# Ten of eleven gated activation chunks transposed by DMAs instead of TensorE

## The chip, the core and the metric

The kernel runs on one core of a Trainium2 chip. The core has five engines that work side by side, each through its own queue in order: TensorE (PE in the profile; its weight loads are PEld), VectorE (DVE), ScalarE (ACT), GpSimd (POOL) and SyncE (SP, which here only issues DMAs). Sixteen DMA engines move data between the main memory and the core's two on-chip memories, SBUF and, for matmul results, PSUM; a DMA can be issued from the queue of SP, ACT or POOL. The metric is the device time of one execution in microseconds; lower is better.

## What is computed

One layer of a decoder block on a sequence of 256 positions with 2048 channels: a mixer with three kinds of attention, then a gated feed-forward part with 5632 hidden channels. All data is 32-bit floating point. The change lies in the feed-forward part:

```python
h2 = rmsnorm(x, g_ffn)
gu = h2 @ w_gu
x = x + (jax.nn.silu(gu[..., :D_FF]) * gu[..., D_FF:]) @ w_down
```

The gated activation, `silu(...) * ...`, has 256 rows (positions) and 5632 columns. It comes out of the first product with positions on the 128 partitions. The second product, with `w_down`, needs it as the stationary operand, with hidden channels on the partitions: it has to be transposed.

## The kernel before

Every product of two 32-bit matrices is made of three matmuls on a rounded 32-bit format: each operand is split into a high half (rounded by a cast on ACT) and a low half (the rest, a subtraction on DVE), and high x high, high x low and low x high are added up in PSUM (`split`, L105; `product`, L158 to L162). Weights are streamed from the main memory in tiles of two 128-row blocks by 512 columns (`load`, L278, and its `fetch` on SP's queue), split by `parts` (L284) into `w_hi` and `w_lo`, of which there are five buffers each, and used by PE. Raw weights have four buffers (`w_raw`) and, for those that are added to each other, six (`g_raw`).

The gate-and-up loop (L933) goes over eleven chunks of 512 hidden channels. `project_pair` (L318) makes the four results of a chunk (two blocks of 128 positions by gate and up). For half of the depth it uses a form of Strassen's scheme with seven products (`form`) in place of eight, for which DVE adds weight tiles to each other (`u`, L303 and L314), and plain products for the other half (`rest`). A chunk takes 22 calls of `parts`, so 22 splits: four for a pair of forms that the previous chunk begins early (`begin_pair`, L308), then two for form 5, one plain, two for form 6, two plain, two for form 7, one plain, two for form 3, two plain, two for form 4, two plain, and the next chunk's four.

After a chunk's products, ACT makes `silu` (L938) and DVE the product with the up part (L939), for two blocks `sg[0]` and `sg[1]` of 128 positions by 512 channels. `to_a` (L925) then transposes each: four PE transposes of 128 x 128 into one PSUM tile (`transpose4`, L178), a copy to SBUF on ACT (L929), and a DMA from POOL's queue to `a_mem` in the main memory (L930), from which the last part of the kernel, the product with `w_down`, reads it back (L950). Small tiles of 2 KB a partition, such as `sg` and these copies, come from one pool of twelve buffers, `scratch`, through `half_kb` (L89).

What is put in between is written as generators: `stages` is a list that `parts` advances by one step at every split, and `slow_stages` one that it advances by one step at every second split (L288 to L291). So `to_a` does one block at the first split of the next chunk's own program and the other at the second.

The order of each engine's queue is not the order of the program: a planner orders the instructions by a simulated timeline, and where several are ready it takes the one that was written first. `tc.keep_in_program_order` binds an instruction behind everything that was written before it for the same engine; what is written later may still overtake it where it is ready sooner.

Of the kernel before, what the change touches and what calls it, by code (L numbers as in the profile page):

```python
# [8 lines left out]

F32 = mybir.dt.float32  # L10
F32R = mybir.dt.float32r
AF = mybir.ActivationFunctionType
ALU = mybir.AluOpType
AX = mybir.AxisListType
# [3 lines left out]
P = 128  # L18
D = 2048
S = 256  # L20
NT = S // P
# [7 lines left out]
NB = 512  # L29
# [25 lines left out]
def hybrid_block(ctx: ExitStack, tc: tile.TileContext, x, g_mix, w_in, q_gain, k_gain, w_branch, w_out,  # L55
                 g_ffn, w_gu, w_down, rel_bias, onehot, extra, out):
    nc = tc.nc
# [21 lines left out]
    def pool(stack, name, side, bufs=1):  # L79
        return stack.enter_context(tc.tile_pool(name=name, bufs=bufs, side=side, reuse_waits="tile"))  # L80
# [5 lines left out]
    scratch = pool(ctx, "scratch", "right", 12)  # L86
    gx = pool(pgx, "gx", "right", 2)

    def half_kb(dt=F32):  # L89

        return scratch.tile([P, NB], dt, name="sc")
# [13 lines left out]
    def split(hi, lo, src, pin=False):  # L105
        for op in nc.scalar.copy(hi, src), nc.vector.tensor_sub(lo, src, hi.bitcast(F32)):  # L106
            if pin:
                tc.keep_in_program_order(op)

    def raw_weights(w, row0, c, col0):  # L110
        raw = wpool.tile([P, 2, NB], F32, name="w_raw", bufs=4)
        src = w[row0 + c * P: row0 + (c + 2) * P, col0: col0 + NB].rearrange("(k p) n -> p k n", p=P)
        return raw, nc.sync.dma_start(raw, src)

    def weights(w, row0, k0, nk, col0, there=()):

        for i, c in enumerate(range(k0, nk, 2)):
            raw = there[i] if i < len(there) else raw_weights(w, row0, c, col0)[0]
            hi = wpool.tile([P, 2, NB], F32R, name="w_hi")
            lo = wpool.tile([P, 2, NB], F32R, name="w_lo")  # L120
            split(hi, lo, raw)
# [4 lines left out]
    stages, slow_stages = [], []  # L126

    def advance(queue):
        while queue:
            try:  # L130
                next(queue[0])
                return
            except StopIteration:
                queue.pop(0)

    def finish_stages(queue):
        while queue:
            advance(queue)
# [25 lines left out]
    def rsqrt_mean(dst, ss, n, cols):  # L164
# [3 lines left out]
        y = small.tile([P, cols], F32, name=f"rs_y{cols}")  # L168
        nc.scalar.activation(y, v, AF.Ln)
        nc.scalar.activation(y, y, AF.Exp, scale=-0.5)  # L170
        t = small.tile([P, cols], F32, name=f"rs_t{cols}")
# [6 lines left out]
    def transpose4(src):  # L178

        pt = tr.tile([P, 4, P], F32, name="tr")  # L180
        for i in range(4):
            nc.tensor.transpose(pt[:, i, :], src[:, i * P:(i + 1) * P], ident)
        return pt


    class Columns:


        def __init__(self, pl, name, nk):
            self.hi, self.lo = (pl.tile([P, nk, S], F32R, name=f"{name}_{n}") for n in ("hi", "lo"))  # L190

# [20 lines left out]
    class Sums:  # L212
# [8 lines left out]
        def place(self, pl, c):  # L221
            self.s[c] = [pl.tile([P, 4, S], F32R, name=f"{self.name}_s{n}{c}") for n in ("hi", "lo")]

# [14 lines left out]
    class Chunks(Sums):  # L238
# [9 lines left out]
        def place(self, pl, c):  # L248
            if c in self.wc:
                super().place(pl, c)  # L250
                self.t[c] = [[pl.tile(sh, F32R, name=f"{self.name}_{t}{n}{c}") for n in ("hi", "lo")]
                             for t, sh in enumerate(([P, 4, P], [P, 2, P]))]
            else:
                self.t[c] = [pl.tile([P, 4, S], F32R, name=f"{self.name}_{n}{c}") for n in ("hi", "lo")]

# [149 lines left out]
    def to_h(acts, src, c, t, g, by_scalar=False):  # L405

        pt = transpose4(src)
        tmp = half_kb().rearrange("p (k q) -> p k q", k=4)
        if by_scalar:
            for i in range(4):  # L410
                nc.scalar.activation(tmp[:, i], pt[:, i], AF.Copy, scale=g[:, 4 * c + i:4 * c + i + 1])
        else:
            nc.vector.tensor_mul(tmp, pt, g[:, 4 * c:4 * c + 4, None].to_broadcast([P, 4, P]))
        acts.put(c, t, tmp)
        return tmp

    def squares(xc, dst, c, pin=False):
        for t in range(NT):
            sq = nc.scalar.activation(half_kb(), xc[t], AF.Square, accum_out=dst[:, t, c:c + 1])
            if pin:  # L420
# [85 lines left out]
    with tc.manual_schedule(engines={mybir.EngineType.PE, mybir.EngineType.DVE, mybir.EngineType.Activation}):  # L506
# [14 lines left out]
        low_high(0, 1)  # L521
        high_low(0, 1)
        turned = [transpose4(xs[1][0])]
        high_high(1, 0)
        high_high(1, 1)
# [7 lines left out]
        high_high(0, 2)  # L533
        low_high(0, 2)
        turned.append(transpose4(xs[1][1]))
        high_high(1, 2)
        low_high(1, 2)
# [89 lines left out]
    def stick_breaking(hl, qT, kT, v):  # L627
# [7 lines left out]
        l = pa.tile([P, n], F32, name="p", bufs=1)  # L635
        nc.scalar.activation(l, z[:, :n], AF.Abs)
        nc.scalar.activation(l, l, AF.Exp, scale=-1.0)
        nc.scalar.activation(l, l, AF.Ln, bias=1.0)
# [160 lines left out]
    def pair_of(kind, what):  # L799
        if kind == "qk":  # L800
            return hs, w_in, what * NB, NH * HD + what * NB
        if kind == "gates":
            return hs, w_in, gate_col(*what[0]), gate_col(*what[1])
# [16 lines left out]
    for (kind, what), after in zip(units, units[1:] + [(None, None)]):  # L820
# [7 lines left out]
        nxt = pair_of(*after)  # L828
# [94 lines left out]
    a_mem = dram.tile([NF // 4, P, 4, S], F32, name="a_mem")  # L923

    def to_a(c, srcs):  # L925
        for t in range(NT):
            pt = transpose4(srcs[t])
            st = half_kb().rearrange("p (k q) -> p k q", k=4)
            nc.scalar.copy(st, pt)  # L929
            nc.gpsimd.dma_start(a_mem[c, :, :, t * P:(t + 1) * P], st)  # L930
            yield

    for c in range(D_FF // NB):  # L933
        nxt = (h2, w_gu, (c + 1) * NB, D_FF + (c + 1) * NB) if c + 1 < D_FF // NB else None
        (g0, g1_, u0, u1), ahead = project_pair(h2, w_gu, c * NB, D_FF + c * NB, ahead, nxt)
        sg = [half_kb() for _ in range(NT)]
        for t, (g, u) in enumerate(((g0, u0), (g1_, u1))):
            nc.scalar.activation(sg[t], g, AF.Silu, scale=rstd2[:, t:t + 1])  # L938
            nc.vector.scalar_tensor_tensor(sg[t], u, rstd2[:, t:t + 1], sg[t], op0=ALU.mult, op1=ALU.mult)  # L939
        stages.append(to_a(c, sg))  # L940

    WD = (4, 6, 8)
    ORDER = [0, 1, 2, 4, 3, 6, 5, 8, 7, 9, 10]
# [153 lines left out]
```

## Time and profile before

| | us |
|---|---|
| median of three runs | 1434.75 |
| lowest and highest | 1433.64, 1435.78 |
| the profiled execution's own time | 1433.64 |
| its span, first to last instruction | 1431.9 |
| PE busy | 1421.7 |
| DVE busy | 1196.0 |
| ACT busy | 882.0 |

A page of the profile lists one execution. A row of a group of instructions has line, engine, operation, tiles (result <- operands), shapes, how many, busy time in us and the mean of one in ns, and then the engine's idle time just before them and what ended it. A row of a timeline has start and duration in us, then the instruction; in brackets the idle time before it and who ended it. Matmuls overlap in their pipeline, so the distance between two starts, not the duration, is what one costs. The loop of the eleven chunks lies from about 735 to 1196 us of the span.

### The profile page before, as it was taken

The page shows a single profiled execution, that of the slowest core. Times are in us where ns is not written, and L with a number is a line of the kernel's source. Part 1 is how long each engine was busy: PE and PEld are TensorE (multiplying, and loading weights), DVE is VectorE, ACT ScalarE, POOL GpSimd, SP SyncE. Part 2 cuts the span into 40 slices and gives each one's busy share as a digit, 9 for nine tenths or more (in the row PEclk, how much of TensorE's full clock was granted, in tenths as well). Part 3 has the DMA queues.
Part 4 walks back from the last instruction along what each step waited for, and adds up shares of the span by engine and source line. Part 5 has one row for each costly group of instructions (what it writes and reads, how often), then busy time and mean ns, then how long its engine had stood idle before and what let it go on. Part 6 is the DMA issues. An engine that isn't in the chain of part 4 may idle for free. (4 is left out here: it accounts for less than half of the span.)

```text
span 1431.9 us, 17773 instructions
## 1 busy us (share of the span) xinstructions
PE 1421.7 (99%) x6404; PEld 1172.1 (82%) x6404; DVE 1196.0 (84%) x1262; ACT 882.0 (62%) x1140; POOL 72.6 (5%) x133
## 2 busy tenths in 40 slices
PE   9999999999999999999999999999999999999998
PEld 7888888888788888888888888888888888788887
DVE  7888787857999886776689999999999998886775
ACT  7667876766766665444456666666666666554453
POOL 1000000000000002100100000000000010100000
PEclk9999999999999999999999999999999999999999
DMA  8763647465666758866786657666665666767552
GB/s 270 264 218 119 220 127 247 122 221 173 215 203 238 257 194 291 278 224 211 223 299 224 224 206 251 216 225 229 219 217 191 231 212 223 256 230 240 190 169 97
DMA packets 154472, 310.09 MB, mean 217 GB/s; under 512 B 10672, under 2 KB 12288, under 8 KB 154384
## 3 DMA queue, kind: packets, MB, share of 16 engines
q1 hardware_dynamic: 143200, 275.29, 57.1%
q0 software_dynamic: 10000, 32.62, 6.5%
q10 hardware_dynamic: 1184, 1.06, 0.2%
q8 instruction: 50, 0.82, 0.2%
q14 instruction: 38, 0.31, 0.1%
HBM read 292.65 MB, written 16.27 MB: 216 GB/s over the span
## 5 line engine op out<-in xcount | busy, mean ns | idle before, releaser
L106 DVE TENSOR_TENSOR w_lo<-w_raw,w_hi 128x1024 fp32r<-128x1024 f32 x334 | 406.0, 1221 | 91.1 <-ACT w_hi L106 87.5
L106 ACT CAST w_hi<-w_raw 128x1024 fp32r<-128x1024 f32 x334 | 349.0, 1052 | 166.1 <-PE qs L162 67.4
L106 ACT CAST w_hi<-g_raw 128x1024 fp32r<-128x1024 f32 x184 | 192.6, 1053 | 120.4 <-PE ps L162 39.4
L106 DVE TENSOR_TENSOR w_lo<-g_raw,w_hi 128x1024 fp32r<-128x1024 f32 x184 | 219.6, 1220 | 36.1 <-ACT w_hi L106 35.2
L106 ACT CAST w_hi<-u 128x1024 fp32r<-128x1024 f32 x138 | 144.9, 1053 | 136.1 <-DVE u L303 65.1
L106 DVE TENSOR_TENSOR w_lo<-u,w_hi 128x1024 fp32r<-128x1024 f32 x138 | 166.5, 1221 | 37.0 <-ACT w_hi L106 35.6
L161 PE MATMUL ps<-w_lo,h_hi 128*128 128x512 f32 x360 | 140.9, 392 | 0.0
L162 PE MATMUL ps<-w_hi,h_lo 128*128 128x512 f32 x360 | 140.5, 390 | 0.0
L160 PE MATMUL ps<-w_hi,h_hi 128*128 128x512 f32 x360 | 137.5, 393 | 0.0
L161 PE MATMUL qs<-w_lo,h_hi 128*128 128x512 f32 x332 | 130.0, 392 | 0.8 <-DVE w_lo L106 0.8
L162 PE MATMUL qs<-w_hi,h_lo 128*128 128x512 f32 x332 | 129.6, 390 | 0.0
L160 PE MATMUL qs<-w_hi,h_hi 128*128 128x512 f32 x332 | 126.7, 391 | 0.0
L303 DVE TENSOR_TENSOR u<-u,g_raw 128x1024 f32<-128x1024 f32 x80 | 94.4, 1218 | 0.0
L162 PEld LDWEIGHTS ps<-w_hi,h_lo 128*128 128x128 f32 x360 | 67.6, 188 | 14.0
L161 PEld LDWEIGHTS ps<-w_lo,h_hi 128*128 128x128 f32 x360 | 67.6, 188 | 13.7
L160 PEld LDWEIGHTS ps<-w_hi,h_hi 128*128 128x128 f32 x360 | 67.5, 188 | 13.7
L161 PEld LDWEIGHTS qs<-w_lo,h_hi 128*128 128x128 f32 x332 | 62.4, 188 | 13.9 <-DVE w_lo L106 1.2
L162 PEld LDWEIGHTS qs<-w_hi,h_lo 128*128 128x128 f32 x332 | 62.4, 188 | 13.4 <-issue 0.6
L160 PEld LDWEIGHTS qs<-w_hi,h_hi 128*128 128x128 f32 x332 | 62.3, 188 | 12.7
L314 DVE TENSOR_TENSOR u<-g_raw 128x1024 f32<-128x1024 f32 x40 | 48.8, 1219 | 21.0 <-DMA g_raw<-in_w_in 16.2
L160 PE MATMUL v<-w_hi,h_hi 128*128 128x512 f32 x120 | 47.5, 396 | 0.2 <-ACT w_hi L106 0.2
L161 PE MATMUL v<-w_lo,h_hi 128*128 128x512 f32 x120 | 47.1, 393 | 0.0
(397 smaller groups left out, 2935.2 us busy)
## 6 DMA issues: line engine op xcount, KB each, us to landing
w_raw<-in_w_in SPq DMA_DIRECT2D x118, 512.0 KB, 4.6
g_raw<-in_w_gu SPq DMA_DIRECT2D x88, 512.0 KB, 5.1
w_raw<-in_w_gu SPq DMA_DIRECT2D x88, 512.0 KB, 6.4
g_raw<-in_w_in SPq DMA_DIRECT2D x72, 512.0 KB, 5.8
w_raw<-in_w_down SPq DMA_DIRECT2D x64, 512.0 KB, 4.6
w_raw<-in_w_branch SPq DMA_DIRECT2D x32, 512.0 KB, 5.1
w_raw<-in_w_out SPq DMA_DIRECT2D x32, 512.0 KB, 4.7
g_raw<-in_w_down SPq DMA_DIRECT2D x24, 512.0 KB, 5.3
```

What stands on the lines that cost most here:

```text
L106: for op in nc.scalar.copy(hi, src), nc.vector.tensor_sub(lo, src, hi.bitcast(F32)):
L160: nc.tensor.matmul(ps, ah, wh, start=start, stop=False, **how)
L161: nc.tensor.matmul(ps, ah, wl, start=False, stop=False, **how)
L162: nc.tensor.matmul(ps, al, wh, start=False, stop=stop, **how)
L303: tc.keep_in_program_order(nc.vector.tensor_add(d, d, a))
L314: nc.vector.tensor_add(d, a, b)
```

## The change

Chunks 0 to 9 are transposed without PE; chunk 10 stays as it was. The transposing DMA is given 16-bit elements: each 32-bit block is handled as two planes of 16-bit halves:

- `turn_out`: a copy on ACT reads the block as 16-bit numbers and writes all first halves of the words to one plane and all second halves to another (128 x 512 x 2); then a transposing DMA, issued from ACT's queue, turns the eight 128 x 128 blocks of the two planes around. Both are bound to program order.
- `turn_in`: a copy on ACT joins the two turned planes into 32-bit words again, bound to program order too. Then POOL stores the block to `a_mem` as before.
- `to_a_by_dma` is put into `slow_stages` in place of `stages`: first block out, two splits later second block out, then two empty steps, then the first block in (eight splits after it went out) and, two splits later, the second.

Three tiles of `scratch` are used for each block in place of one. Before the last chunk's `to_a`, `slow_stages` is run to its end.

```diff
+U16 = mybir.dt.uint16
...
+    def turn_out(src):
+
+        halves = scratch.tile([P, 2, NB], U16, name="sc")
+        tc.keep_in_program_order(nc.scalar.copy(halves, src.bitcast(U16).rearrange("p (n b) -> p b n", b=2)))
+        turned = scratch.tile([P, 8, P], U16, name="sc")
+        tc.keep_in_program_order(nc.scalar.dma_start_transpose(turned, halves.rearrange("p b n -> p (b n)")))
+        return turned
+
+    def turn_in(turned):
+
+        dst = half_kb().rearrange("p (k q) -> p k q", k=4)
+        tc.keep_in_program_order(nc.scalar.copy(dst.bitcast(U16).rearrange("p k (q b) -> p b k q", b=2),
+                                                turned.rearrange("p (b k) q -> p b k q", b=2)))
+        return dst
...
+    def to_a_by_dma(c, srcs):
+        turned = []
+        for t in range(NT):
+            turned.append(turn_out(srcs[t]))
+            yield
+        yield
+        yield
+        for t in range(NT):
+            nc.gpsimd.dma_start(a_mem[c, :, :, t * P:(t + 1) * P], turn_in(turned[t]))
+            yield
...
-        stages.append(to_a(c, sg))
+        if nxt:
+            slow_stages.append(to_a_by_dma(c, sg))
+        else:
+            finish_stages(slow_stages)
+            stages.append(to_a(c, sg))
```

## The prediction

> **What bounds the kernel now.** First the page: which engine has no idle time.
>
> ```profile
> span 1431.9 us, 17773 instructions
> PE 1421.7 (99%) x6404; PEld 1172.1 (82%) x6404; DVE 1196.0 (84%) x1262; ACT 882.0 (62%) x1140; POOL 72.6 (5%) x133
> ```
>
> PE is never free, so only work taken from PE, or a wait put on it, moves the time. The transposes in question run in the gate-and-up loop of eleven chunks (L933). So next the stretches of that view, one for each chunk; this is one of them, with its columns.
>
> ```profile
> core 0: us, PE busy (x) PEld busy (x) DVE busy (x) ACT busy (x) POOL busy (x), PEclk, DMA share, GB/s
> 986.70:1028.40 41.70, 41.70 (x190) 34.57 (x189) 38.82 (x36) 26.58 (x31) 1.46 (x2) 1.00 0.63 215
> ```
>
> A chunk takes 41.7 us, all PE. DVE is busy 38.8 of it, 93%, and can make up for little; ACT 26.6. PE is fed by a chain: ACT casts a pair of weight rows to its high half (L106), DVE subtracts to get the low half, PE multiplies. There are 22 such splits in a chunk and five buffers for the halves, so what matters is how far ahead the chain is at the place where the change puts its work. I number the splits of a chunk's program from the cast of u after the two pairs begun early: 1 and 2 are u for form 5, 3 a plain row pair, 4 and 5 the new u for form 6, and so on. The timelines of the three engines there (start, duration):
>
> ```profile
> 986.80 0.72 ACT L938 ACTIVATE sc<-sc,rstd 128x512 f32<-128x512 f32 x1
> 987.43 0.67 ACT L938 ACTIVATE sc<-ps,rstd 128x512 f32<-128x512 f32 x1
> 988.00 1.04 ACT L106 CAST w_hi<-u 128x1024 fp32r<-128x1024 f32 x1
> 988.93 0.58 ACT L298 COPY sc<-qs 128x512 f32<-128x512 f32 x1
> 989.48 1.05 ACT L106 CAST w_hi<-w_raw 128x1024 fp32r<-128x1024 f32 x1
> 992.86 0.59 ACT L929 COPY sc<-tr 128x512 f32<-128x512 f32 x1 [2.33 <-PE tr L182]
> 993.34 1.05 ACT L106 CAST w_hi<-u 128x1024 fp32r<-128x1024 f32 x1
> 994.29 0.59 ACT L929 COPY sc<-tr 128x512 f32<-128x512 f32 x1
> 994.77 1.06 ACT L106 CAST w_hi<-u 128x1024 fp32r<-128x1024 f32 x1
> ...
> 988.08 1.41 DVE L939 SCALAR_TENSOR_TENSOR sc<-sc,rstd 128x512 f32<-128x512 f32 x2
> 989.40 1.22 DVE L106 TENSOR_TENSOR w_lo<-u,w_hi 128x1024 fp32r<-128x1024 f32 x1
> 990.57 1.23 DVE L106 TENSOR_TENSOR w_lo<-w_raw,w_hi 128x1024 fp32r<-128x1024 f32 x1
> 991.71 2.36 DVE L303 TENSOR_TENSOR u<-u,g_raw 128x1024 f32<-128x1024 f32 x2
> 994.43 1.23 DVE L106 TENSOR_TENSOR w_lo<-u,w_hi 128x1024 fp32r<-128x1024 f32 x1 [0.36 <-ACT w_hi L106]
> ...
> 995.88 0.39 PE L160 MATMUL qs<-w_hi,h_shi 128*128 128x512 f32 x1
> 996.10 0.39 PE L161 MATMUL qs<-w_lo,h_shi 128*128 128x512 f32 x1
> ```
>
> Split 4 is cast at 993.34, its low half ends at 994.43 + 1.23 = 995.66, and PE reads it at 996.10. **The lead is 0.44 us**, here, just behind the two activations that the change turns out. ACT's one large hole, 2.33 us up to 992.86, lies here too; it is a wait for PE's transposes.
>
> **What is taken away.** Ten chunks lose eight transposes each. In order of time on PE:
>
> ```profile
> 992.23 0.60 PE L182 MATMUL tr<-ident,sc 128*128 128x128 f32 x4
> 992.58 0.48 PE L160 MATMUL z<-w_hi,h_shi 128*128 128x512 f32 x1
> 992.90 0.60 PE L182 MATMUL tr<-ident,sc 128*128 128x128 f32 x4
> 993.25 0.48 PE L160 MATMUL v<-w_hi,h_hi 128*128 128x512 f32 x1
> 993.57 0.40 PE L161 MATMUL z<-w_lo,h_shi 128*128 128x512 f32 x1
> ```
>
> From 992.23 to 993.57 are 1.34 us with two matmuls in them; matmuls follow each other every 0.226 us (995.88 to 996.10). The eight transposes therefore hold PE 1.34 − 0.45 = 0.89 us, and ten chunks 8.9 us. That is all there is to gain. ACT loses two copies a chunk, at a pitch of 0.48 (994.29 to 994.77), and no longer waits for PE.
>
> **What is added on ACT.** Per chunk two copies into planes, two transposing DMAs issued from ACT's own queue, and two copies that join the planes. No such copy is in this trace. It has 1024 elements of 16 bits: the rows above give 0.59 for 512 elements and 1.05 for 1024, so 0.59 if time goes with bytes, 1.05 if with elements. I take 1.05 (0.95 in pitch, 988.00 to 988.93): the two 128x512 forms and the 128x1024 cast lie on one line in the count of elements. ACT's total per chunk becomes 26.6 − 1.0 + 4 × 0.95 = 29.4 and is no bound by itself.
>
> The DMA is the open price. It stands in program order right behind the copy whose result it reads, on the same queue, so ACT cannot start the next cast until the copy has ended and the DMA is issued. I call that hold h. The rows nearest to it are plain DMAs:
>
> ```profile
> L1065 ACTq DMA_DIRECT2D out<-sc x8: 338/338/369, 1307.1 to 1428.6; - x8
> L103 SPq DMA_DIRECT2D g_raw<-in_w_gu x10: 367/368/838, 981.1 to 1024.0; - x10
> L930 POOL DMA_DIRECT2D a_mem<-sc x22: 709/713/825, 785.3 to 1207.2; - x22
> ```
>
> ACT's own stores are 128 runs of 1 KB and take 0.338 us to issue, SP's loads 256 runs of 2 KB and 0.368. A transposed half tile has 128 rows of eight blocks, each block going to another plane: 1024 runs. Straight through the two rows that is 0.338 + 7 × 0.030 = 0.55; in proportion to SP's runs 4 × 0.368 = 1.47. POOL's store of 512 runs, at 0.713, lies between the two lines. To each comes the end of the copy that the DMA waits for, some 0.2, an estimate from the 0.44 between the copy's end at 993.45 and the store's start at 993.89 on another engine:
>
> ```profile
> 993.89 0.73 POOL L930 DMA_DIRECT2D a_mem<-sc  x1 [35.98 <-ACT sc L929]
> ```
>
> So h lies between 0.34 (the plain issue alone) and about 1.7. I take 1.47 + 0.2 = 1.67: by the number of its runs, 1024, the transpose is nearest to SP's row of 256, and a row whose every run goes on to the next address may be cheap for a reason that a transpose does not share.
>
> [...]
>
> **How it adds up at split 4.** Without transposes PE would read split 4's low half 0.89 earlier, at 995.21. ACT now does, after the snapshot that starts at 988.93 (next free at 989.45): copy, hold, cast of split 3, copy, hold. Three pitches of 0.95 and two holds end at 992.3 + 2h, where split 4 can start; not before 992.9 though, when DVE has its first sum of u (991.71 + half of 2.36). Against 993.34 now that is a delay of 2h − 1.04. PE's reading moves by this delay less the lead of 0.44: **each chunk changes by 2h − 1.48 us, and by −0.89 at best**. Break-even is h = 0.74. With 1.67 a chunk is 1.86 us longer, of which PE waits 2.75.
>
> A second order of the same work: if the first copy and its DMA stand ahead of split 3's cast, split 3's low half slips by 0.95 + h, DVE's sums of u behind it in its queue slip as well, and split 4 starts at about 993.85 + h; the chunk changes by h + 0.07, or 1.74 with 1.67. For a long hold both orders agree, and I need not know which one the planner chose.
>
> **What is added later in the chunk.** The joining copies stand behind splits 9 and 11:
>
> ```profile
> 1000.70 2.19 ACT L106 CAST w_hi<-g_raw 128x1024 fp32r<-128x1024 f32 x2 [1.08 <-DVE g_raw L303]
> 1002.78 1.05 ACT L106 CAST w_hi<-w_raw 128x1024 fp32r<-128x1024 f32 x1
> 1003.74 1.04 ACT L106 CAST w_hi<-g_raw 128x1024 fp32r<-128x1024 f32 x1
> 1005.64 1.05 ACT L106 CAST w_hi<-g_raw 128x1024 fp32r<-128x1024 f32 x1 [0.85 <-ACT w_hi L106]
> 1006.98 0.39 PE L160 MATMUL v<-w_hi,h_hi 128*128 128x512 f32 x1
> ```
>
> Split 10 (cast at 1002.78, low half done 2.5 us later, at 1005.28) is first read by PE at 1006.98: a lead of 1.70 against one copy of 0.95. I cost both joins at nothing; if the lead were gone, they would cost up to 1.9 a chunk. Queued behind a join that has to wait for its DMA would be every cast to come, and so DVE and PE. The cover is about 12 us, from an issue near 990.5 to 1002.8. Nearest rows, medians from issue to landing in this stage:
>
> ```profile
> w_raw<-in_w_gu SPq DMA_DIRECT2D x76, 512.0 KB, 6.2
> a_mem<-sc POOLq DMA_DIRECT2D x20, 256.0 KB, 2.5
> ```
>
> 2.5 to 6.2 us fit into 12, so I cost the landing at nothing. [...] POOL's stores to a_mem are the same twenty, some 9 us later; their reader for chunk 9 comes a whole chunk later. The DMA engines are at 0.63 of their time in the chunk and get twice 256 KB more. The twelve scratch buffers have about six holders at this place, so no buffer is late.
>
> **The sum.** 10 × 1.86 = +18.6 on the profiled execution's own 1433.64 us (its span is 1431.9): 1452.2. The median of the runs before is 1434.75, 1.1 above it: **1453 us**.
>
> **Rivals.** *A short hold (the other side).* The issue costs what a plain one costs, h = 0.34 to 0.6, split 3 goes first, and PE keeps most of the 0.89: −1.48 + 2h is −0.80 to −0.28, in ten chunks −8 to −3, 1427 to 1432 us; −8.9 at best. It decides from h below 0.74. For it: issuing hardly grows with bytes (0.338 and 0.368), and ACT's hole of 2.33 us is free for it. Against: the copy's end must be waited for, and the runs are eight times as many.
>
> *A short hold, first copy ahead of split 3.* h + 0.07 with 0.55 is +0.6, ten times +6: 1441. With h near 0.2 it is no change.
>
> *The transposes land late, or hold up the weights.* DMA is full just when they start:
>
> ```profile
> 989.00:991.00 2.00, 2.00 (x10) 1.65 (x10) 2.00 (x3) 1.54 (x3) 0.00 (x0) 1.00 0.98 369
> 991.00:993.00 2.00, 2.00 (x13) 1.65 (x12) 2.00 (x3) 0.14 (x1) 0.00 (x0) 1.00 0.37 132
> ```
>
> If landing took 20 us, ACT would stand 8 us before the first join, PE 8 − 1.7 = 6.3, ten chunks 63 us on top of −8.9 to +19: about 1490 to 1520. It decides from a landing above some 13.7 us. Against it: the share falls to 0.37 from 991 on.
>
> **Chances.** A hold of 1.2 to 2.2 us (each chunk +0.9 to +2.9, so 1444 to 1464): 0.45, the forecast. The short hold with a gain: 0.27, of which 0.03 is too small to see. The short hold behind the other order: 0.13, of which 0.05 no change. Late landing or weights held up: 0.15. A measurement of this kernel tells 0.2%, 2.9 us, from no change. Faster 0.24, the same 0.08, slower 0.68. The range reaches down to most of the short hold, 1427, and up to 1482, the forecast's upper end plus a little of the late landing (1.8 us a chunk); the forecast's own is 1444 to 1464.
>
> **What would show it.** On ACT's queue, the duration of the transposing DMA against 1.47 and the time from the copy's start to the next cast against 0.95 + 1.67; PE waiting some 2.7 us a chunk for w_lo at split 4 and no transposes beside it; DVE idle for ACT there; nothing before the joins. I am wrong if PE does not wait at split 4 (then h is short), or if ACT waits for a DMA before the joins.

## The result

| | us |
|---|---|
| before, median of 11 runs | 1434.06 (1432.63 to 1435.78) |
| after, median of 11 runs | 1437.53 (1436.36 to 1439.12) |
| ratio after to before | 1.0024, 95% interval 1.0015 to 1.0034 |
| forecast | 1453, range 1427 to 1482 |
| the profiled execution of after: own time, span | 1439.12, 1437.4 |

The change makes the kernel slower, by 3.5 us where 18.6 were forecast: the direction and the place were right, the size was five times too large, and the two holds that were to cost it cost little. The page of the changed kernel, span and engines:

```profile
span 1437.4 us, 17633 instructions
PE 1417.3 (99%) x6324; PEld 1162.1 (81%) x6324; DVE 1192.7 (83%) x1262; ACT 914.1 (64%) x1160; POOL 72.6 (5%) x133
```

PE has 80 instructions less, worth 8.9 us by the prediction's count, and the span is 5.5 us longer than the 1431.9 of before: PE waits some 14 us more in the profiled execution, the longest of the eleven; by the medians it is some 12. Where it does is seen in any chunk. The timeline of ACT in one of them (start, duration; in brackets the idle time before and who ended it), then DVE and PE, and last a row of ACT in the chunk of before that the prediction shows:

```profile
946.57 0.72 ACT L965 ACTIVATE sc<-sc,rstd 128x512 f32<-128x512 f32 x1
...
948.93 1.05 ACT L107 CAST w_hi<-w_raw 128x1024 fp32r<-128x1024 f32 x1 [0.60 <-DMA w_raw<-in_w_gu]
949.89 1.04 ACT L189 COPY sc<-sc 128x1024 uint16<-128x1024 uint16 x1
950.96 1.25 ACTq L191 DMA_TRANSPOSE sc<-sc  x1
952.25 0.59 ACT L314 COPY sc<-z 128x512 f32<-128x512 f32 x1 [1.32 <-PE z L163]
952.73 1.05 ACT L189 COPY sc<-sc 128x1024 uint16<-128x1024 uint16 x1
953.68 1.05 ACT L107 CAST w_hi<-u 128x1024 fp32r<-128x1024 f32 x1
953.81 1.25 ACTq L191 DMA_TRANSPOSE sc<-sc  x1
...
954.76 2.36 DVE L107 TENSOR_TENSOR w_lo<-u,w_hi 128x1024 fp32r<-128x1024 f32 x2 [1.25 <-ACT w_hi L107]
...
951.76 0.39 PE L163 MATMUL z<-w_hi,h_slo 128*128 128x512 f32 x1
...
954.78 0.51 PE L161 MATMUL ps<-w_hi,h_shi 128*128 128x512 f32 x1
956.04 0.50 PE L162 MATMUL ps<-w_lo,h_shi 128*128 128x512 f32 x1 [0.76 <-DVE w_lo L107]
...
996.66 0.60 ACT L298 COPY sc<-z 128x512 f32<-128x512 f32 x1
```

In neither of the two orders that the prediction considered does the snapshot of `z` (L314) have a part. Here it stands ahead of the first cast of `u` (split 4), and the second copy into planes stands between the two; in that chunk of before (996.66) it came behind the casts of splits 4 to 6. The snapshot can start only when PE has ended form 5, whose last matmul into `z` starts at 951.76. From there the chain to PE's next low half is fixed: 0.49 to the snapshot, 0.48 for it, 0.95 for the copy, 1.08 to DVE, 1.28 to PE, which is 4.28 us, to 956.04. PE meanwhile has the twelve matmuls of split 3 and one of split 4, fourteen steps of 0.226 or 3.16 us. It waits for the difference, about 1.1 us: the last step, 954.78 to 956.04, takes 1.26 us where 0.226 is usual. This step, 1.26 us or about 1.03 beyond the usual, stands in every one of the ten chunks. Without the copy's 0.95 it would all but vanish.

The hold behind the first DMA is real: its copy ends at 950.93 and the next instruction starts at 952.25, 1.32 us later. But ACT would have waited there for `z` anyway: PE sets the snapshot at 5.61 us behind the chunk's first activation where it sets it alone (four chunks of the ten), and here it comes at 5.68, 0.04 behind the end of the issue. The hold has just used up its cover, the wait that ACT has there in any case. The second DMA (953.81) is issued while ACT casts on; in its queue it stands behind the casts of splits 4 to 7, and holds up nothing. The issues (ns) and landings (us) of all chunks, each with least, median and most, by their source line, then the group of the joins (in all, us, and the mean, ns, then ACT's idle time in front of them):

```profile
L191 ACTq DMA_TRANSPOSE sc<-sc x20: 1247/1248/1394, 782.6 to 1166.4; - x20
...
DMA to landing us min/median/max: 2.7/4.8/7.2
```

```profile
L197 ACT COPY sc<-sc 128x1024 uint16<-128x1024 uint16 x20 | 27.2, 1360 | 0.0
```

An issue takes 1.25 us, a landing 2.7 to 7.2, a copy into planes 1.04 (949.89), a join 1.36; ACT is never idle in front of a join (0.0), so no landing is late.

### The profile page after: what moved, and what is told of

It is laid out like the page before. It is cut to its first block, busy times and chain, and to the rows that moved or that the text cites. A ratio compares the mean times of both kernels' runs of the same rounds, so it can differ in the third digit from the quotient of the medians.

```text
span 1437.4 us, 17633 instructions
## 1 busy us (share of the span) xinstructions
PE 1417.3 (99%) x6324; PEld 1162.1 (81%) x6324; DVE 1192.7 (83%) x1262; ACT 914.1 (64%) x1160; POOL 72.6 (5%) x133
## 4 chain that ended last, share of the span: by engine, by line
PE 63%; DVE 10%; DMA 6%; issue 4%; ACT 4%; ACTq 1%; SPq 0%; DVEq 0%; POOLq 0%
PE ps L162 7%; PE ps L163 7%; PE ps L161 7%; PE qs L162 7%; PE qs L163 7%; PE qs L161 7%; DVE w_lo L107 6%; DMA w_raw<-in_w_gu 3%; PE z L161 3%; PE z L162 3%; PE z L163 3%; ACT w_hi L107 2%; PE v L161 2%; PE v L162 2%; PE v L163 2%
## 5 line engine op out<-in xcount | busy, mean ns | idle before, releaser
L161 PE MATMUL z<-w_hi,h_hi 128*128 128x512 f32 x120 | 47.0, 392 | 0.6 <-ACT sc L314 0.6
L319 DVE TENSOR_TENSOR g_raw<-g_raw 128x1024 f32<-128x1024 f32 x40 | 47.0, 1217 | 0.0
```

Of the source, the lines that this page charges most:

```text
L161: nc.tensor.matmul(ps, ah, wh, start=start, stop=False, **how)
L319: tc.keep_in_program_order(nc.vector.tensor_add(d, d, a))
```

## The experiments

All were timed in five rounds beside the kernel before, 4 to 12 executions each, with a median of 1434.3 for before. Edits are against the changed kernel. Where a copy or a transposing DMA is left out, the block that is stored is not transposed.

| run | what differs from the changed kernel | median, us | ratio to before, 95% |
|---|---|---|---|
| e1 | no copies, no DMAs | 1425.6 | 0.9942 (0.993 to 0.9955) |
| e2 | copies, no DMAs | 1435.01 | 1.0008 (1.0 to 1.0017) |
| e3 | plain DMAs for the transposing ones | 1435.73 | 1.0012 (1.0003 to 1.0021) |
| e4 | two steps later | 1431.3 | 0.998 (0.9971 to 0.9989) |
| e5 | second block one step later | 1434.11 | 0.9995 (0.9986 to 1.0004) |
| e6 | DMAs, no copies | 1431.49 | 0.9991 (0.9978 to 1.0004) |
| e7 | three steps later | 1434.66 | 1.0006 (0.9997 to 1.0015) |
| e8 | five steps later | 1431.88 | 0.9989 (0.9975 to 1.0003) |
| e9 | first block's DMA twice | 1449.78 | 1.0109 (1.0095 to 1.0123) |
| e10 | e5 without the DMAs | 1432.92 | 0.9994 (0.9985 to 1.0003) |
| e11 | one step later | 1433.12 | 0.9993 (0.9985 to 1.0002) |
| e12 | e4 with the joins on GpSimd | 1442.7 | 1.0065 (1.0051 to 1.0078) |

**What each part costs: e1, e2, e3.**

```diff
 # e1
-            turned.append(turn_out(srcs[t]))
+            turned.append(srcs[t])
...
 # e2: the join reads `halves`
-        tc.keep_in_program_order(nc.scalar.dma_start_transpose(turned, halves.rearrange("p b n -> p (b n)")))
-        return turned
+        return halves
...
 # e3
-        tc.keep_in_program_order(nc.scalar.dma_start_transpose(turned, halves.rearrange("p b n -> p (b n)")))
+        tc.keep_in_program_order(nc.scalar.dma_start(turned.rearrange("p k q -> p (k q)"), halves.rearrange("p b n -> p (b n)")))
```

> Leaves out the transposing of chunks 0 to 9 altogether: the gated blocks are stored as they are, so PE's 80 transposes are gone and nothing is put in their place. Theory A (PE reads split 4's low half 0.44 us after it is ready; with ACT free its cast can start 0.44 earlier): a chunk loses the whole 0.89, ten 8.9: about 1425.5 against 1434.1, and PE waits for nothing at split 4. Rival B (DVE, 93% busy, is the bound as soon as PE has less to do): half of it or less, 1430 or more, with PE waiting for w_lo in every chunk.

> The change with its four copies a chunk and without its transposing DMAs (the joining copy reads the planes that were not turned). ACT's queue keeps its order. Theory A (the hold of 1.33 us behind the first copy is what makes split 4 late): split 4's cast starts 1.33 earlier, where it is not late any more; the chunk keeps nearly all of 0.89: 1426 to 1428. Rival C (the copies' time on ACT is what costs): 1434 to 1437. Rival D (the DMAs' traffic makes weights late): falls as well, to 1426 to 1430, and the chunks with a wait for w_raw lose it.

> The change with plain DMAs of the same 256 KB from the same place in ACT's queue instead of transposing ones; the planes are not turned. Theory A: the hold falls from 1.33 to about 0.4 (a plain issue takes 0.34 to 0.37), split 4 is 0.9 earlier: 1427 to 1429. Rival D (traffic of 512 KB more a chunk): as the traffic stays, most of the change's loss stays: 1434 to 1437.

With nothing done the kernel takes 1425.6 us, 8.7 below before: the transposes' 0.89 us a chunk is right, and no other engine stops PE from gaining it. The windows of one chunk of e1 (PE, PEld, DVE, ACT, POOL busy, clock, DMA share, GB/s):

```profile
982.27:1023.07 40.80, 40.80 (x182) 33.81 (x181) 38.56 (x36) 25.64 (x29) 1.48 (x2) 1.00 0.64 217
```

A chunk is 40.80 us, all of it PE. With the copies alone, e2, 9.4 us come back, against an expectation that the hold was what cost. Without any DMA PE steps 1.26 us at the same place in nine chunks of ten, and 1.03 in the other, because the second copy still stands there. From e2's timeline of ACT:

```profile
1030.36 0.72 ACT L963 ACTIVATE sc<-sc,rstd 128x512 f32<-128x512 f32 x1
...
1035.97 0.59 ACT L312 COPY sc<-z 128x512 f32<-128x512 f32 x1 [1.96 <-PE z L163]
1036.45 1.05 ACT L189 COPY sc<-sc 128x1024 uint16<-128x1024 uint16 x1
```

ACT is idle 1.96 us for `z` where the hold of 1.32 lay: the cover has 0.64 us to spare. The snapshot comes 5.61 us behind the first activation here and 5.68 in the chunk of after that was shown, so the hold moves next to nothing there. Plain DMAs (e3) add 0.7 us to e2, less than the intervals tell apart, and the transposing ones 2.5. The time of e3 is the one expected if traffic costs, but e2 takes as long without any of that traffic. Their issues and landings in e3:

```profile
L191 ACTq DMA_DIRECT2D sc<-sc x20: 472/472/518, 783.3 to 1163.9; - x20
...
DMA to landing us min/median/max: 2.2/2.5/4.3
```

In the profiled executions (spans 1433.5 for e2, 1437.4 for after) the difference lies in three chunks of the ten: 42.9 to 44.0 us from one activation to the next, where the others are 41.98 to 42.20. In these three, split 3's weights come 1.3 to 1.8 us late and use up the spare 0.64. From after's timeline of ACT:

```profile
1034.05 1.05 ACT L107 CAST w_hi<-w_raw 128x1024 fp32r<-128x1024 f32 x1 [1.68 <-DMA w_raw<-in_w_gu]
...
1036.07 1.25 ACTq L191 DMA_TRANSPOSE sc<-sc  x1
1037.36 0.59 ACT L314 COPY sc<-z 128x512 f32<-128x512 f32 x1 [1.32 <-issue]
```

Here the wait ahead of the snapshot is no longer ended by PE but by the issue itself. e4, timed with these three (below), took 1431.3 us with all the work kept. These results made a new theory: **what stands in ACT's queue between the snapshot of `z` and split 4's cast is paid by PE, whatever it is, and a hold ahead of the snapshot is free as long as ACT would wait there for PE anyway.**

**A hold that has no cover: e9.**

```diff
         tc.keep_in_program_order(nc.scalar.dma_start_transpose(turned, halves.rearrange("p b n -> p (b n)")))
+        if twice:   # first block only
+            again = scratch.tile([P, 8, P], U16, name="sc")
+            tc.keep_in_program_order(nc.scalar.dma_start_transpose(again, halves.rearrange("p b n -> p (b n)")))
```

> The first block's transposing DMA is issued twice (the second time into another scratch tile that nothing reads); all else as in the changed kernel. On ACT's queue two issues of 1.25 us stand between the first copy and the snapshot of z. Theory E (one hold is free only because ACT would wait there for PE to end form 5, about 1.3 us): the second issue finds no wait left to hide in, the snapshot and the cast of split 4 come 1.25 us later, PE's step at split 4 grows from 1.26 to about 2.5, ten chunks 12.5 us: 1448 to 1452. Rival G (issuing a DMA never holds up ACT's casts, it goes on beside them): 1437 to 1440.

1449.8 us, within the expectation, 12.3 above the changed kernel for ten issues. The place differs from the expectation. ACT's timeline, then PE's:

```profile
1000.55 1.26 ACTq L191 DMA_TRANSPOSE sc<-sc  x1
1001.86 1.36 ACTq L194 DMA_TRANSPOSE sc<-sc  x1
1003.25 0.59 ACT L317 COPY sc<-z 128x512 f32<-128x512 f32 x1 [2.73 <-issue]
...
1002.53 0.39 PE L163 MATMUL v<-w_hi,h_lo 128*128 128x512 f32 x1
1003.89 0.50 PE L161 MATMUL z<-w_hi,h_hi 128*128 128x512 f32 x1 [0.97 <-ACT sc L317]
...
1005.79 0.50 PE L161 MATMUL qs<-w_hi,h_shi 128*128 128x512 f32 x1 [0.23 <-ACT w_hi L107]
1007.05 0.50 PE L162 MATMUL qs<-w_lo,h_shi 128*128 128x512 f32 x1 [0.76 <-DVE w_lo L107]
```

The step at split 4 is 1.26 us as before. What the second hold adds falls earlier: PE waits for the snapshot itself, which has to empty `z` before split 3 may write to it (1002.53 to 1003.89, 1.36 us; 0.71 to 1.67 in the ten chunks). The snapshot is the hinge on both sides.

**The same work in two orders within one kernel: e6 and e11.**

```diff
 # e6: the DMA reads the block itself, nothing reads its result, the block is stored as it is
-        halves = scratch.tile([P, 2, NB], U16, name="sc")
-        tc.keep_in_program_order(nc.scalar.copy(halves, ...))
-        tc.keep_in_program_order(nc.scalar.dma_start_transpose(turned, halves.rearrange("p b n -> p (b n)")))
+        tc.keep_in_program_order(nc.scalar.dma_start_transpose(turned, src.bitcast(U16)))
...
 # e11
         turned = []
+        for _ in range(1):
+            yield
```

> No copy into planes and no join: the transposing DMAs read the block itself, their result is not used, and the block is stored as it is. On ACT's queue the second DMA now stands between the snapshot of z and the cast of split 4. Theory E: its issue, about 1.3 us with the step to the next instruction, takes the place of the copy's 0.95; PE waits about 1.3 to 1.4 us a chunk at split 4; 10 x 1.35 on the 1425.6 of the kernel with nothing done, plus some 2.5 for the DMAs' traffic: 1438 to 1442. The snapshot of z still waits for PE, so the first DMA costs nothing. Rival F (the copies are what costs, a DMA issued from ACT is hidden anyway): 1426 to 1430.

> All the work of the change, one empty step ahead of the first block's going out. On ACT's queue split 4's cast now stands ahead of the snapshot of z, and the first copy between that snapshot and split 5's cast. Theory E: nothing that waits for PE, and no copy, stands ahead of split 4 any more, so no 1.26 us step there; what split 5 loses, 0.95, is about its lead: 1427 to 1432. Rival (the second cast of u pays in place of the first): 1435 to 1438.

Both totals miss the ranges (1431.5 lies between the theories, 1433.1 just above its range), since the planner did not choose one order for all chunks. That lets two orders of the same work be compared within one execution. e6, ACT and a row of DVE in an early chunk, ACT in a later one:

```profile
831.69 0.59 ACT L309 COPY sc<-z 128x512 f32<-128x512 f32 x1 [2.90 <-PE z L163]
831.75 1.25 ACTq L189 DMA_TRANSPOSE sc<-sc  x1
833.10 1.05 ACT L107 CAST w_hi<-u 128x1024 fp32r<-128x1024 f32 x1 [0.82 <-DVE u L314]
...
829.96 2.35 DVE L314 TENSOR_TENSOR u<-u,g_raw 128x1024 f32<-128x1024 f32 x2
...
1040.87 1.05 ACT L107 CAST w_hi<-u 128x1024 fp32r<-128x1024 f32 x1 [2.50 <-DVE u L314]
1040.92 1.45 ACTq L189 DMA_TRANSPOSE sc<-sc  x1
1041.82 0.58 ACT L309 COPY sc<-z 128x512 f32<-128x512 f32 x1
```

In the early order the issue stands between the snapshot and split 4's cast. The bracket names DVE, but the first of its two sums was there at 831.14 and the second at 832.31; the issue lasts to 833.00. PE steps 1.25 to 1.26 us, in four chunks. In the later order the cast stands ahead of both, and in the six chunks that have it no step is longer than 0.73. (e6's first chunk loses 4 us more, where ACT waits 4.29 us for a block read back from `a_mem`.) e11, with the copy in place of the issue:

```profile
911.44 0.59 ACT L314 COPY sc<-z 128x512 f32<-128x512 f32 x1 [2.83 <-PE z L163]
911.93 1.05 ACT L189 COPY sc<-sc 128x1024 uint16<-128x1024 uint16 x1
912.87 1.05 ACT L107 CAST w_hi<-u 128x1024 fp32r<-128x1024 f32 x1
...
953.40 1.06 ACT L107 CAST w_hi<-u 128x1024 fp32r<-128x1024 f32 x1 [2.50 <-DVE u L319]
954.36 0.59 ACT L314 COPY sc<-z 128x512 f32<-128x512 f32 x1
954.83 1.06 ACT L189 COPY sc<-sc 128x1024 uint16<-128x1024 uint16 x1
```

The four chunks with the first order are 41.98 to 42.38 us long and have the step of 1.26; the six with the second 40.87 to 41.52, with no step above 0.5. In e6 and e11 alike the first order lies in the first four chunks and the second in the last six. The place in the loop is not what makes the 1 us: in e1, where nothing stands between and the order changes at the same chunk, the first two chunks take 41.0 us and the fifth to the eighth 40.8.

**Moving it out of the way: e4, e5, e7, e8, e10.**

```diff
 # e4, e7, e8: n is 2, 3, 5
         turned = []
+        for _ in range(n):
+            yield
...
 # e5: one step between the blocks; e10: the same, and the join reads `halves` as in e2
-        for t in range(NT):
-            turned.append(turn_out(srcs[t]))
-            yield
+        turned.append(turn_out(srcs[0]))
+        yield
+        yield
+        turned.append(turn_out(srcs[1]))
```

> The change with two empty steps ahead of the first copy, so that both copies and both DMAs come four splits later, behind the casts of splits 4 and 5, where the chain has more lead. All work is kept. Theory A (it is the place: 0.44 us of lead at split 4): PE waits no more at split 4, and the removal of the transposes shows: 1426 to 1430, faster than before. Rival C (ACT's work) and rival D (traffic): the same work and the same traffic, so within 2 us of the change's 1437.5.

> All the work of the change stays; only the second block's copy and DMA come one step later (out 0, empty, out 1). On ACT's queue the second copy no longer stands between the snapshot of z, which waits for PE to end form 5, and the casts of split 4 and 5, but behind these casts. Theory E (what stands between that snapshot and the cast of split 4 is paid by PE in full, whatever it is, and nothing else of the change costs much): one copy less there is 0.95 us a chunk, 10 x 0.95 = 9.5 off the changed kernel's 1437.5, so 1428 to 1430, and the 1.26 us step of PE at split 4's low half shrinks to under 0.4. Rival F (the four copies a chunk cost wherever they stand, by ACT's time or by SBUF traffic beside DVE): 1436 to 1439.

> All the work of the change, three empty steps ahead of the first block's going out: on ACT's queue snapshot of z, casts of splits 4 to 7, the next snapshot, then the copies and DMAs among the casts of form 7's weights. Theory E: nothing stands between the snapshot of z and split 4, so no 1.26 us step there; 1426 to 1431, faster than before, unless the next splits have no more lead than split 4. Rival F: 1436 to 1439.

> All the work of the change, five empty steps ahead: copies and DMAs stand behind the snapshot of the ninth and tenth split, between casts of plain weight rows. Theory E: 1426 to 1431 again; which of the two late places is better it doesn't say. Rival F: 1436 to 1439.

> As the kernel with the second copy one step later, without the transposing DMAs: the joins read the planes themselves, the output is not the reference's. In that kernel ACT waits 1.0 to 1.5 us for the weights of split 3, and PE still steps 0.72 at split 4. Theory W1 (the transposing DMAs' traffic makes those weights late): ACT's wait at split 3 falls under 0.4, the step goes, 1427 to 1430. Theory W2 (the weights are simply the next limit when PE comes some 1 us earlier): the waits stay, 1432 to 1435.

None of them has the step of 1.26 us at split 4, and all are below the changed kernel; but only e4 is clearly below before, and of the four that keep all the work none came within its expected range: e4 and e8 lie some 1 us above it, e5 and e7 some 4. The theory names the place of the loss, not the whole time. e5 gained 3.4 us of the 9.5 expected. ACT's timeline of one chunk, then PE's:

```profile
944.84 0.72 ACT L966 ACTIVATE sc<-sc,rstd 128x512 f32<-128x512 f32 x1
...
947.85 1.05 ACT L107 CAST w_hi<-w_raw 128x1024 fp32r<-128x1024 f32 x1 [1.25 <-DMA w_raw<-in_w_gu]
...
949.87 1.25 ACTq L191 DMA_TRANSPOSE sc<-sc  x1
951.16 0.59 ACT L314 COPY sc<-z 128x512 f32<-128x512 f32 x1 [1.32 <-PE z L163]
...
953.29 0.39 PE L161 MATMUL ps<-w_hi,h_shi 128*128 128x512 f32 x1
954.02 0.50 PE L162 MATMUL ps<-w_lo,h_shi 128*128 128x512 f32 x1 [0.34 <-DVE w_lo L107]
```

ACT waits 1.25 us for split 3's weights; copy and hold follow so late that the issue ends at 951.12 and sets the snapshot, 6.32 us behind the activation. In the two chunks whose weights are under 0.3 late it comes after 5.61, set by PE; in the other eight after 6.0 to 6.9. So the hold outlasts its cover, and PE steps 0.73. The bracket that names PE `z` there is a case of a wait put down to the wrong one of two. e10, without DMAs, has the snapshot at 5.6 to 5.7 in every chunk, and yet only 1.2 us of e5's time come back, which the intervals do not tell from nothing. The weights are as late there, 0.8 to 2.0 us in nine chunks of ten. e10, ACT, then a row of ACT in e5 from behind the loop:

```profile
988.74 1.05 ACT L107 CAST w_hi<-w_raw 128x1024 fp32r<-128x1024 f32 x1 [1.48 <-DMA w_raw<-in_w_gu]
...
992.28 2.18 ACT L107 CAST w_hi<-u 128x1024 fp32r<-128x1024 f32 x2 [0.58 <-DVE u L317]
...
1219.89 1.04 ACT L107 CAST a_hi<-a_raw 128x1024 fp32r<-128x1024 f32 x1 [2.87 <-DMA a_raw<-a_mem]
```

Now split 4 waits for DVE's sum of `u`, which stands behind split 3's low half and so behind its weights. So it is not the transposes' traffic that makes them late. That they are only the next limit, met because PE comes earlier (the second of the two theories), fits the total but is not shown: in e5 and e10 SP issues the fetch of these weights 3.6 to 3.8 us ahead of the chunk's first activation in nine chunks of ten, in the changed kernel 4.0 to 4.3 us ahead, and what delays it was not tried. e7's wait for the same weights is 1.0 to 2.1 us in six chunks; e4's is 0.7 to 1.3 in eight. Why e4 does better than e7 was not tried either.

Part of what e5 and e10 miss lies behind the loop. In the profiled executions the loop, from the first chunk's first activation to the last chunk's, takes 416.9 us in e5 and 415.4 in e10, where the changed kernel takes 424.5 and before 418.2. But from there to the end e5 takes 237.3 us and e10 237.7, where the changed kernel takes 235.5 and before 235.7 (e7 236.9, e8 239.1, e4 234.8). In the product with `w_down` ACT waits 2.87 us for a block read back from `a_mem` (1219.89; 3.64 us in e10), and the cast of a sum of weights that PE needs next stands behind it: PE waits 1.84 us (1.78 in e10). The loop itself gained more than the totals of e5 and e10 say.

e8 shows one thing more. Its joins start 8 to 9 us after the issue of their DMAs in seven chunks, where the changed kernel has 11.7 or more, and two landings are late. ACT's timeline:

```profile
841.51 1.25 ACTq L191 DMA_TRANSPOSE sc<-sc  x1
...
855.06 1.33 ACT L197 COPY sc<-sc 128x1024 uint16<-128x1024 uint16 x1 [4.58 <-DMA sc<-sc]
```

ACT stands 4.58 us in front of a join, 13.5 us after its DMA was issued, and PE's longest step in that chunk is 3.18. The late landing that was a rival exists, where the cover is shorter; why these two landings took 13.5 and 12.9 us was not tried.

**The joins elsewhere: e12.**

```diff
 # on e4
-        tc.keep_in_program_order(nc.scalar.copy(dst.bitcast(U16)...
+        tc.keep_in_program_order(nc.gpsimd.tensor_copy(dst.bitcast(U16)...
```

> The faster version with two empty steps, its two joining copies a chunk on GpSimd in place of ACT. Theory E (the joins are not on PE's path): no change against that version's 1431.3, 1429 to 1433. Rival (ACT's total time in the chunk still costs): 1425 to 1428. Rival (GpSimd's copies slow DVE's or come late for the store): 1435 or more.

11.4 us worse than e4. DVE, then POOL:

```profile
960.08 3.46 DVE L319 TENSOR_TENSOR g_raw<-g_raw 128x1024 f32<-128x1024 f32 x2
...
966.93 3.46 DVE L107 TENSOR_TENSOR w_lo<-g_raw,w_hi 128x1024 fp32r<-128x1024 f32 x2
...
959.74 1.64 POOL L197 COPY sc<-sc 128x1024 uint16<-128x1024 uint16 x1 [32.31 <-DMA sc<-sc]
...
967.25 2.12 POOL L197 COPY sc<-sc 128x1024 uint16<-128x1024 uint16 x1 [4.71 <-DMA sc<-sc]
```

A pair of DVE instructions takes 3.46 us beside one of POOL's copies, where a pair takes 2.36 elsewhere (954.76 in the changed kernel). At the two joins of that chunk one DVE instruction takes 2.32 us instead of 1.22. In the whole execution these two groups, the sums into `g_raw` and the low halves of `g_raw`, take 58.0 and 229.4 us, where e4 has 47.1 and 218.6: 21.7 us for twenty joins. DVE loses 1.1 us for each join and has, at 93% of a chunk, little room for it. So e12 does not tell whether the joins cost anything on ACT. At both the stretched DVE instruction ends 1.02 us after POOL's copy has ended (962.40 after 961.38, 970.39 after 969.37); what holds it up was not tried.

## Why the prediction was right in direction and wrong in size and cause

- **PE bounds, and the transposes are worth 0.89 us a chunk**: right. 8.9 us forecast, 8.7 measured (e1).
- **PE waits for the low half at split 4**: right in place, in every chunk. 2.75 us were forecast, 1.03 is the usual size, and the cause is a copy, not the holds.
- **The step that failed** is "Three pitches of 0.95 and two holds end at 992.3 + 2h, where split 4 can start". It added up ACT's own work from the last snapshot on as if nothing in that queue waited for PE; the prediction says so itself, ACT "no longer waits for PE". The planner put the snapshot of `z` ahead of split 4's cast, so the count for split 4 starts when PE ends form 5 and not when ACT has finished its own work. What stands ahead of the snapshot (a cast, a copy, the first hold) vanishes in ACT's wait for PE, up to 1.96 us without the DMA (e2); what stands behind it, one copy of 0.95, is paid. The second hold was counted too, though casts of four splits stand between the copy and its DMA. In the profiled execution the holds delay the snapshot by 0.23 us or less in seven chunks and by 0.96 to 1.27 in the three whose weights are late, 3.9 us in all ten; its span is 3.9 us longer than that of e2.
- **The hold itself**: 1.32 us, of which 1.25 is the issue, forecast 1.67 and 1.47. With 1.32 the prediction's formula would still give 2 × 1.32 − 1.48 = 1.16 a chunk, 11.6 in all; the size alone does not explain the miss.
- **The sum as the runs have it**: −8.7 (e1), +9.4 for the copies in their place (e1 to e2), +2.5 for the DMAs (e2 to after): +3.2; measured +3.5. Each term is the distance from one run to the next, so they add up by construction; what speaks for the cause is the place of the step in each run.
- **The direction**: right, in part by luck. In the prediction's formula a chunk without holds gains 0.89, and only the holds make it slower. The runs have it the other way: the copies take the whole gain back without any DMA (e2).
- **Copies into planes at 1.05**: right, 1.04. **Joins at nothing**: right as far as PE's steps show it; a join takes 1.36, not 1.05, and PE's steps of over 0.5 us all lie in the first 10 us of a chunk, the joins behind 15.
- **The landing fits its cover**: right, 4.8 in the median and 7.2 at most in a cover of 12. The transposing DMA is still the slower one: the plain DMA of the same tile in e3 lands in 2.5 us and is issued in 0.47, where the transposing one takes 1.25 to issue.
- **The short hold as a rival** came nearest to the cover with "ACT's hole of 2.33 us is free for it". That hole is a wait for PE's transposes, which the change takes away; the cover in the runs is another, ACT's wait for `z`, 1.96 us (e2). It hides a hold of 1.32 as well as a short one, unless the weights are late.

e4 beats both kernels with all the work of the change done: 1431.3 us, 0.2% below before.

## What to carry to other kernels

Before adding up what an in-order queue will do, find the instruction in it that waits for the bounding engine: what is put ahead of it is free up to the length of that wait, here 1.96 us (e2). What is put between it and the next piece of work that the bounding engine needs is paid where that engine has no lead: here a copy of 0.95 us (e2) and the issue of a DMA, 1.25 us (e6), both made PE's step 1.26 us where 0.226 is usual. Place new work by that instruction, not by the total of the engine, which here stood at 64%. And where a planner sets the order, look at the order of the new kernel, chunk by chunk: it can differ between chunks of one loop.

## What was not expected of the hardware

In the changed kernel a transposing DMA of 128 x 1024 elements of 16 bits from SBUF to SBUF takes 1.25 us to issue and a median of 4.8 to land, where in e3 a plain one of the same tile and place takes 0.47 and 2.5. The 16-bit copy that writes with a stride (the join) takes 1.36 us and the one that reads with a stride 1.04, for the same number of elements. In the chunk of the changed kernel that was shown, the second DMA stands in ACT's queue behind the casts of splits 4 to 7, and is issued at 953.81; of these, the casts that start at 953.68 and 954.63 run beside the issue. In e6's early chunk the DMA stands ahead of split 4's cast and waits for no copy; the cast starts at 833.10, 0.10 after the issue has ended.
